# A hybrid encoder block on one core: two centred LayerNorm cells kept on chip, new lane rates, a fifth raw weight buffer, and roots a call later

## The chip, the cores and the metric

The kernel runs on one NeuronCore of a Trainium2 chip. Its engines are named here as the profile names them: TensorE (PE, its weight loads PEld), VectorE (DVE), ScalarE (ACT), GpSimd (POOL) and SyncE (SP), which issues most DMAs. The metric is the device time of one execution, in microseconds (us).

## The reference

One layer over 2048 tokens of 1024 channels, in float32:

```
h = rmsnorm(x)
u_pool(512) | u_glu(2x512) | g_a(1024) | g_b(1024) = h @ w_in
A = ((trailing_mean(u_pool, 2/4/8/16) - u_pool) @ pool_w per group * pool_scale) @ w_pool_out
v = depthwise_conv31(a * sigmoid(gate)) + conv_b            # 512 channels, causal
B = silu(layernorm(v) * ln_g + ln_b) @ w_conv_out
x = x + rmsnorm((sigmoid(g_a) * A + sigmoid(g_b) * B) @ w_o)
x = x + rmsnorm(relu(rmsnorm(x) @ w_up)^2 @ w_down)
```

## The kernel before

**Number format and tiling.** Every float32 operand is split into a high and a low half of a faster format (`split`, `split_w`: ScalarE casts the high half, VectorE subtracts for the low one), and three of the four half products are summed. Each matrix product of 2 x 2 blocks is done with seven block products and sums of blocks (`Octet`, products numbered 1 to 7, in the sequence `START`, then `ORDER`). One such product is 24 matmuls of 128x128 by 128x512 into one accumulator of 1024 columns in PSUM. There are 385 of them: glu, pool, ga and gb (the input projection), A and B (the two branches), wo, up and down. Tokens go in two halves of 1024 (`b` = 0, 1).

**Weights.** `load_w` loads a raw weight tile into a buffer of pool `wr` (four), ScalarE casts it to `wh`. The low half `wl` is made by VectorE at first use and stored in DRAM (`kept`); at the second use it is loaded from there, `wl<-kept`.

**What sets the order.** TensorE runs the products in one main line. Other work is written as generators (`conv_steps`: 31 depthwise taps, one VectorE instruction each, L918; `pool_steps`; `norm_steps`, the LayerNorm; `pool_weights`, which folds w_pool into w_pool_out; `mlp_scale`, the sums of squares for the mlp's norm). A `Lane` calls them after each product: its `rate` is added to a credit, each step costs one, and a `yield n` has the lane skip n - 1 calls. Within `behind()` each instruction of a step is bound not to be placed before the main line's last one. The scheduler lays out each engine's instructions in an order fixed in the program; `high_priority(offset=...)` brings instructions forward in it. An engine runs its list in order and waits at the first instruction that is not ready. So do the DMA queues: SP's list holds nearly all loads and most stores (`load`, L129), ScalarE's some stores (`store`, L137), POOL's a few transfers (`aside`, and those that accumulate).

**The norm.** `norm_steps` subtracts the mean from four cells (a cell is 128 channels by 1024 tokens), stores each centred cell to DRAM (`yd`), sums squares, has TensorE make the root's sum (`root_acc`, L458) and spread it, loads the four cells again, and makes z, which goes to DRAM as `zd`. z is the operand of the B products. `yd` also carries the convolution's result to the norm.

**Roots.** A root is eight or sixteen matmuls of one column, put between TensorE's product matmuls. `mlp_scale` runs for the second half while the up products run; its squares lie in buffers named fo.

**Sums.** Every second product or so, a sum of two accumulators is made: ScalarE copies one out of PSUM (`held`, L408), VectorE adds the other (`tr<-gb,tr`, L120), and the accumulator is free again after that. Three accumulators exist.

Of the kernel before, what the change touches and what calls it, by code (L numbers as in the profile page):

```python
# [15 lines left out]
P = 128  # L16
# [52 lines left out]
def block_kernel(  # L69
# [20 lines left out]
    p_const = pool("const", 1)  # L90
    p_dram = pool("dram", 1, space=bass.MemoryType.DRAM)
    p_sm = pool("psm", 2)
    p_wr = pool("pwr", 4)
    p_ws = pool("pws", 2)
    p_wh = pool("pwh", 3)
    p_wl = pool("pwl", 3)
# [31 lines left out]
    def load(o, src):  # L128
        return nc.sync.dma_start(o, src)  # L129
# [308 lines left out]
                self.sink(1, 0, ps, None)  # L438
            bg()

    def run_octets(octets, bg):

        jobs = [(octets[k], i) for k, i in START]
        jobs += [(o, i) for o in octets[2:] for i in ORDER]
        for n, (o, i) in enumerate(jobs):
            o.run(i, jobs[min(n + (2 if n > 3 else 1), len(jobs) - 1)][1], bg)
            if n == 3:
                o.raw.clear()

# [446 lines left out]
    def conv_steps(b, groups, ahead=True):  # L896
# [8 lines left out]
        for c in groups:  # L905
# [24 lines left out]
            load(yd[b, c, 0], acc)  # L930
            yield

    def norm_steps(b, lag):

        yield 3
        sh, sl = split(sums[b], *TR)
        yield 3
        mu = mk(p_ss, "r", F32, (P, W))[:, :TB]
        y = {}

        def prefetch(c):
# [12 lines left out]
        ss = mk(p_ss, "sm")  # L954
        for c in range(CC):
            if c + 2 < CC:
                prefetch(c + 2)
            sub(y[c], y[c], mu)
            load(yd[b, c, 0], y[c])
            sq = ss if c == 0 else tr()  # L960
            nc.scalar.activation(sq, y[c], AF.Square)
            if c % 2:
                yield 1
            if c:
                add(ss, ss, sq)
        yield lag
        r = mk(p_ss, "r", F32, (P, W))[:, :TB]
        halves = [ss[:, t * T : (t + 1) * T] for t in (0, 1)]

        def got(t, rb):  # L970
            nc.scalar.copy(r[:, t * T : (t + 1) * T], rb)

        yield from inv_rms_steps(halves, inv_c, TR, lag, got)
        prefetch(0)
        yield 1
        sg = {}
        for c in range(CC + 1):
            if c < CC:
                if c + 1 < CC:
                    prefetch(c + 1)  # L980
                mul(y[c], y[c], r)
                sg[c] = tr()
                nc.scalar.activation(
                    sg[c], y[c], AF.Sigmoid, scale=col(C_LG + c), bias=col(C_LB + c)
                )
                nc.scalar.activation(
                    y[c], y[c], AF.Identity, scale=col(C_LG + c), bias=col(C_LB + c)
                )
            if c:
                mul(y[c - 1], y[c - 1], sg[c - 1])  # L990
                load(zd[b, c - 1, 0], y[c - 1])
            yield 1

    pw = [p_const.tile([P, CW], F32R, tag=f"pw{i}", name=f"pw{i}") for i in (0, 1)]

    w_pp = [dram("wpp", (P, D)) for _ in range(CPS)]

    def pool_weights():

        yield 2  # L1000
        raw = tr()
        load(raw[:, :CW], w_pool)
        for g in range(CC):
            part = raw[:, g * P : (g + 1) * P]
            nc.scalar.activation(part, part, AF.Copy, scale=col(C_PSC + g))
        nc.scalar.copy(pw[0], raw[:, :CW])
        sub(pw[1], raw[:, :CW], f32(pw[0]))
        yield

        def get(g):  # L1010
            t = tr()
            load(t, w_po[g])
            return t

        for g, t in ahead_by_one(range(CC), get):
            hi, lo = split(t, *TR)
            yield 3
            ps = psum("mix")
            for h in (0, 1):
                n = slice(h * T, (h + 1) * T)  # L1020
                matmuls(ps[:, n], pw, g, [(hi[:, n], lo[:, n])], main=False)
            w = tr()
            nc.scalar.copy(w, ps)
            yield
            for c in range(CPS):
# [346 lines left out]
    def mlp_scale(b, buf):  # L1372

        st = None
        for t in (0, 1):
            sq = Squares(buf)
            for c in range(0, CPS, 2):
                x = [mk(*buf) for _ in (0, 1)]
                for i in (0, 1):
                    load(x[i], x1d[b, c + i, t])  # L1380
                yield 1
                sq.add(x[0])
                sq.add(x[1])
            yield 1
            ss = sq.total()
            yield 1
            if st is None:
                st = root_psum()
            root_acc(st, ss, inv_d, t * G)
# [8 lines left out]
    def mlp_up(b, parts):  # L1398
        def one(u):
# [3 lines left out]
            def sink(m, t, ps, s):  # L1403
                o = tr()
                if s is not None:
                    mark(add(o, ps, s))
                    ps = o
                mark(nc.scalar.activation(o, ps, AF.Relu))
                nc.scalar.activation(o, o, AF.Square)
# [74 lines left out]
            lane.empty()  # L1484
        lanes.clear()

    def run(*octets):
        run_octets([o for group in octets for o in group], bg)

    parts = Parts(first_parts)  # L1490
    first_octet()
    parts.need(6)
    o2, = glu(0, parts, ahead_raw[:1])
    tail = Lane(1.3, conv_steps(0, (0,)))
    stats = Lane(1, in_stats(1))
    weights = Lane(2, pool_weights())

    def then(f, o, at=4):
# [20 lines left out]
    then(lambda: lanes.append(stats), o2, 5)  # L1519
    run(  # L1520
        [o2],
        [then(more, pi, 3)],
        gate(0, parts, 3, sad, "ga", "lows"),
        gate(0, parts, 5, sbd, "gb", "sums"),
    )
    stats.empty()
    weights.empty()
# [19 lines left out]
    def pooling():  # L1547
# [9 lines left out]
        g1[0],  # L1557
        g1[1],
        gate(1, parts, 5, sbd, "gb", "sums"),
    )  # L1560
    conv1 = lanes.pop()
    empty()
# [224 lines left out]
    class Finish:  # L1787
# [144 lines left out]
        for i in FIRST:  # L1932
            fill[i] = token_cells(0, i, 0, (p_fo, "fo"))

    def filler(part):
        for i in FIRST:
            for o in (0, 1):
                w = part(i, o)
                ps = psum("down")
                product(ps, w, fill[i])  # L1940
# [18 lines left out]
    filler(weights_down(0))  # L1959
# [5 lines left out]
    run(octs)  # L1965
    empty()
    part = {}
    coming = got
# [97 lines left out]
```

## Time and profile before

| | us |
|---|---|
| median of 3 executions (lowest to highest) | 2214.71 (2211.72 to 2218.5) |
| the profiled execution | 2215.49 |
| its span, first to last instruction | 2213.7 |
| TensorE busy | 2165.7 |
| VectorE busy | 1677.5 |
| ScalarE busy | 1040.2 |
| moved by DMA | 567.51 MB, mean 256 GB/s |

The profile is of one execution. A row of the timeline gives the start, the length, the engine, the line, the instruction as out<-in, how many were merged into the row, and, in brackets, how long the engine stood idle before and what released it. The list of waits gives a sum, how many, and the longest. The table of stretches gives, for each, its length, the busy time and count of each engine shown, the granted TensorE clock (PEclk), the share of DMA engines busy and GB/s; where one engine alone is asked for, the first pair is that engine's.

### The profile page before, as it was taken

The page shows a single profiled execution, that of the slowest core. Times are in us where ns is not written, and L with a number is a line of the kernel's source. Part 1 is how long each engine was busy: PE and PEld are TensorE (multiplying, and loading weights), DVE is VectorE, ACT ScalarE, POOL GpSimd, SP SyncE. Part 2 cuts the span into 40 slices and gives each one's busy share as a digit, 9 for nine tenths or more (in the row PEclk, how much of TensorE's full clock was granted, in tenths as well). Part 3 has the DMA queues.
Part 4 walks back from the last instruction along what each step waited for, and adds up shares of the span by engine and source line. Part 5 has one row for each costly group of instructions (what it writes and reads, how often), then busy time and mean ns, then how long its engine had stood idle before and what let it go on. Part 6 is the DMA issues. An engine that isn't in the chain of part 4 may idle for free.

```text
span 2213.7 us, 25020 instructions
## 1 busy us (share of the span) xinstructions
PE 2165.7 (98%) x9556; PEld 1784.4 (81%) x9556; DVE 1677.5 (76%) x1633; ACT 1040.2 (47%) x1098; POOL 20.6 (1%) x39
## 2 busy tenths in 40 slices
PE   9999999999999999999999999999999999999996
PEld 7788787887888788888888877888888888888875
DVE  8998998987778888967657856876754656696667
ACT  5444353334533445456535766664554222223553
POOL 0000000000000000000000000000000000000001
PEclk9999999999999999999999999999999999999998
DMA  4779897678986688365686677985966545446798
GB/s 166 275 291 344 305 366 282 236 278 310 351 323 238 252 311 310 123 218 189 229 306 236 247 267 266 329 317 197 372 213 233 181 156 189 149 146 219 266 319 248
DMA packets 162791, 567.51 MB, mean 256 GB/s; under 512 B 18896, under 2 KB 23120, under 8 KB 162640
## 3 DMA queue, kind: packets, MB, share of 16 engines
q1 hardware_dynamic: 145968, 505.09, 64.1%
q10 hardware_dynamic: 12672, 46.14, 5.3%
q0 software_dynamic: 4032, 14.68, 2.5%
q8 instruction: 75, 1.23, 0.2%
q14 instruction: 44, 0.36, 0.0%
HBM read 376.49 MB, written 190.41 MB: 256 GB/s over the span
## 4 chain that ended last, share of the span: by engine, by line
PE 76%; DVE 9%; DMA 9%; issue 2%; ACT 2%; SPq 0%; DVEq 0%; ACTq 0%; POOL 0%; POOLq 0%
PE down L252 26%; PE up L252 22%; PE glu L252 6%; PE wo L252 6%; PE B L252 4%; PE A L252 4%; PE ga L252 3%; PE gb L252 3%; PE pool L252 2%; DVE y L918 2%; DVE wl L123 1%; DMA tr<-yd 1%; DVE tr L120 1%; DMA fo<-x1d 1%; DMA kept<-ws 1%
## 5 line engine op out<-in xcount | busy, mean ns | idle before, releaser
L252 PE MATMUL up<-big,wh 128*128 128x512 f32 x1792 | 482.4, 390 | 2.1 <-DVE big L123 1.8
L252 PEld LDWEIGHTS up<-big,wh 128*128 128x128 f32 x1792 | 337.0, 188 | 74.5 <-DVE big L123 3.9
L209 ACT CAST wh<-wr 128x1024 fp32r<-128x1024 f32 x169 | 177.5, 1051 | 324.1 <-PE up L252 77.8
L252 PE MATMUL down<-tr,wh 128*128 128x512 f32 x800 | 311.7, 390 | 0.0
L918 DVE SCALAR_TENSOR_TENSOR y<-v,cst,y 128x1024 f32<-128x1024 f32 x240 | 307.3, 1281 | 2.8
L252 PE MATMUL down<-fo,wh 128*128 128x512 f32 x784 | 301.8, 390 | 0.0
L252 PE MATMUL up<-big,wl 128*128 128x512 f32 x896 | 277.2, 390 | 0.0
L252 PE MATMUL down<-fo,wl 128*128 128x512 f32 x768 | 236.8, 390 | 2.9 <-DMA wl<-lows 2.9
L209 ACT CAST wh<-ws 128x1024 fp32r<-128x1024 f32 x118 | 124.2, 1052 | 221.8 <-PE up L252 84.1
L252 PEld LDWEIGHTS up<-big,wl 128*128 128x128 f32 x896 | 168.3, 188 | 34.7
L120 DVE TENSOR_TENSOR big<-big,down 128x1024 f32<-128x1024 f32 x88 | 106.8, 1218 | 111.9 <-PE down L252 104.0
L1727 ACT CAST fo<-tr 128x1024 fp32r<-128x1024 f32 x86 | 86.8, 1051 | 210.0 <-PE down L252 132.1
L252 PEld LDWEIGHTS down<-tr,wh 128*128 128x128 f32 x800 | 150.6, 188 | 31.2
L252 PEld LDWEIGHTS down<-fo,wh 128*128 128x128 f32 x784 | 147.5, 188 | 30.6
L252 PEld LDWEIGHTS down<-fo,wl 128*128 128x128 f32 x768 | 144.1, 188 | 33.2 <-DMA wl<-lows 3.3
L123 DVE TENSOR_TENSOR wl<-ws,wh 128x1024 fp32r<-128x1024 f32 x110 | 134.2, 1220 | 32.7 <-ACT wh L209 31.5
L123 DVE TENSOR_TENSOR wl<-wr,wh 128x1024 fp32r<-128x1024 f32 x99 | 120.5, 1218 | 27.9 <-ACT wh L209 26.8
L123 DVE TENSOR_TENSOR tr<-tr,fo 128x1024 fp32r<-128x1024 f32 x86 | 101.8, 1220 | 46.5 <-ACT fo L1727 46.5
L252 PE MATMUL wo<-big,wh 128*128 128x512 f32 x480 | 128.9, 390 | 0.0
L252 PE MATMUL gb<-big,wh 128*128 128x512 f32 x448 | 121.0, 392 | 3.0 <-DVE tr L120 2.4
L252 PE MATMUL glu<-big,wh 128*128 128x512 f32 x432 | 120.2, 400 | 3.5 <-DVE big L123 1.8
L252 PE MATMUL ga<-big,wh 128*128 128x512 f32 x448 | 120.9, 392 | 0.0
(197 smaller groups left out, 3349.1 us busy)
## 6 DMA issues: line engine op xcount, KB each, us to landing
tr<-fd SPq DMA_DIRECT2D x110, 512.0 KB, 4.6
wl<-kept SPq DMA_DIRECT2D x81, 512.0 KB, 4.8
kept<-wl SPq DMA_DIRECT2D x74, 512.0 KB, 5.7
wr<-w_down SPq DMA_DIRECT2D x68, 512.0 KB, 5.2
wr<-w_up SPq DMA_DIRECT2D x64, 512.0 KB, 4.6
wr<-w_in SPq DMA_DIRECT2D x56, 512.0 KB, 5.4
fd<-tr ACTq DMA_DIRECT2D x54, 512.0 KB, 3.6
fd<-tr SPq DMA_DIRECT2D x48, 512.0 KB, 3.5
```

The lines of the kernel that those rows point to most:

```text
L120: return nc.vector.tensor_tensor(o, a, b, op=ALU.add)
L123: return nc.vector.tensor_tensor(o, a, b, op=ALU.subtract)
L209: nc.scalar.copy(hi[:, :n], src[:, :n])
L252: i = nc.tensor.matmul(ps, w[wp][:, (at + k) * P : (at + k + 1) * P], rhs[k][xp], start=start and n == 0, stop=stop and n == len(order) - ...
L918: nc.vector.scalar_tensor_tensor(acc, v[:, k : k + TB], wk, acc, op0=ALU.mult, op1=ALU.add)
L1727: nc.scalar.copy(hi, t)
```

## The change

- Pool `wr` of raw weights has five buffers instead of four.
- `norm_steps` keeps the centred cells 2 and 3 on chip (HELD): they are neither stored to `yd` nor loaded again. The second pass takes them first, then cells 0 and 1, which it asks for up to two ahead.
- The two halves of w_pool, constants before, are a temporary of one `tr` buffer, and `pool_weights` skips a call more.
- `mlp_scale` skips one call more before its root, and `mlp_up`'s sum of two accumulators is scheduled with an offset of 60.
- The convolution's lane starts after glu's second octet (`o2`) has done its product 1, one product later than before, at rate 1 instead of 1.3, later 2.5 instead of 3; the rest of its work is appended two products earlier. The second half's lane goes to 2.2 instead of 3.4.
- `run_octets` takes from which product on it looks two products ahead for operands: 3 as before, but 2 in the last `mlp_up`.
- The plain `out` store in `mul_left` goes through POOL's queue instead of SP's.

No instruction of TensorE, VectorE or ScalarE is added or removed. Eight transfers of 0.5 MB go.

```diff
-    p_wr = pool("pwr", 4)
+    p_wr = pool("pwr", 5)
...
-    def run_octets(octets, bg):
+    def run_octets(octets, bg, early):
...
-            o.run(i, jobs[min(n + (2 if n > 3 else 1), len(jobs) - 1)][1], bg)
+            o.run(i, jobs[min(n + (2 if n > early else 1), len(jobs) - 1)][1], bg)
...
+    HELD = (CC - 2, CC - 1)
+
     def norm_steps(b, lag):
...
             sub(y[c], y[c], mu)
-            load(yd[b, c, 0], y[c])
+            if c not in HELD:
+                load(yd[b, c, 0], y[c])
...
         yield from inv_rms_steps(halves, inv_c, TR, lag, got)
-        prefetch(0)
+        order = HELD + tuple(c for c in range(CC) if c not in HELD)
+        ready = list(HELD)
+
+        def ask(n):
+            if n < CC and order[n] not in ready:
+                prefetch(order[n])
+                ready.append(order[n])
+
+        ask(0)
         yield 1
         sg = {}
-        for c in range(CC + 1):
-            if c < CC:
-                if c + 1 < CC:
-                    prefetch(c + 1)
+        for n in range(CC + 1):
+            if n < CC:
+                c = order[n]
+                ask(n + 1)
+                ask(n + 2)
                 mul(y[c], y[c], r)
...
-            if c:
-                mul(y[c - 1], y[c - 1], sg[c - 1])
-                load(zd[b, c - 1, 0], y[c - 1])
+            if n:
+                c = order[n - 1]
+                mul(y[c], y[c], sg[c])
+                load(zd[b, c, 0], y[c])
             yield 1
-
-    pw = [p_const.tile([P, CW], F32R, tag=f"pw{i}", name=f"pw{i}") for i in (0, 1)]
...
         raw = tr()
+        both = mk(*TR, F32R)
+        pw = both[:, :CW], both[:, CW:]
...
             hi, lo = split(t, *TR)
-            yield 3
+            yield 4
...
             ss = sq.total()
-            yield 1
+            yield 2
             if st is None:
                 st = root_psum()
             root_acc(st, ss, inv_d, t * G)
...
                 if s is not None:
-                    mark(add(o, ps, s))
+                    with tc.high_priority(offset=60):
+                        mark(add(o, ps, s))
...
-    tail = Lane(1.3, conv_steps(0, (0,)))
+    tail = Lane(1, conv_steps(0, (0,)))
...
+    def after_glu():
+        ahead[0] = AHEAD
+        lanes.append(tail)
+
     def more():
         ahead[0] = AHEAD
         lanes.append(weights)
         tail.gens.append(chain_of(pool_steps(0, True), conv_steps(0, (1, 2, 3), False)))
-        tail.rate = 3
+        tail.rate = 2.5
...
     ahead[0] = 45
-    lanes.append(tail)
     then(lambda: lanes.append(stats), o2, 5)
     run(
-        [o2],
-        [then(more, pi, 3)],
+        [then(after_glu, o2, 1)],
+        [then(more, pi, 5)],
...
     def faster():
-        conv1.rate = 3.4
+        conv1.rate = 2.2
...
-                    load(out[self.b, c, self.t], y)
+                    nc.gpsimd.dma_start(out[self.b, c, self.t], y)
...
-    run(octs)
+    run(octs, early=2)
```

The other lines of the diff pass `early=3`, or hand the fill-in products of down their weights as arguments, with the same work.

The scheduler's order shows what moves. VectorE, the gb products of the first half (y is the convolution's accumulator, wl a low weight half, ws a sum of weights). Before:

```order
L120 TENSOR_TENSOR tr_2084<-gb_2058,tr_2046 128x1024
L123 TENSOR_TENSOR wl_2189<-ws_2186,wh_2188 128x1024
L918 SCALAR_TENSOR_TENSOR y_2005<-v_1957,cst,y_2005 128x1024 x3
L123 TENSOR_TENSOR ws_2227<-wr_2051,ws_2097 128x1024
L918 SCALAR_TENSOR_TENSOR y_2005<-v_1957,cst,y_2005 128x1024 x2
L123 TENSOR_TENSOR wl_2230<-ws_2227,wh_2229 128x1024
L918 SCALAR_TENSOR_TENSOR y_2005<-v_1957,cst,y_2005 128x1024 x2
L123 TENSOR_TENSOR wl_2269<-wr_2093,wh_2268 128x1024
L918 SCALAR_TENSOR_TENSOR y_2005<-v_1957,cst,y_2005 128x1024 x2
L120 TENSOR_TENSOR tr_2220<-gb_2020,tr_2181 128x1024
```

With the change:

```order
L120 TENSOR_TENSOR tr_2073<-gb_2047,tr_2028 128x1024
L123 TENSOR_TENSOR wl_2162<-ws_2159,wh_2161 128x1024
L123 TENSOR_TENSOR ws_2213<-wr_2040,ws_2084 128x1024
L914 TENSOR_SCALAR y_2156<-v_2119,cst 128x1024
L123 TENSOR_TENSOR wl_2216<-ws_2213,wh_2215 128x1024
L918 SCALAR_TENSOR_TENSOR y_2156<-v_2119,cst,y_2156 128x1024
L123 TENSOR_TENSOR wl_2254<-wr_2080,wh_2253 128x1024
L120 TENSOR_TENSOR ws_2371<-wr_2367,wr_2369 128x1024
L123 TENSOR_TENSOR ws_2373<-ws_2371,wr_2290 128x1024
L120 TENSOR_TENSOR tr_2193<-gb_2002,tr_2154 128x1024
```

Between the first and the second add of gb stand nine taps before, and two steps of the convolution with the change.

SP's queue where the first half's last products (A, pool) end and those of the second begin (kept, wsum and the like are in DRAM). Before:

```order
L129 DMA wl_2990<-kept_795 128x1024
L129 DMA wr_3188<-kept_1256 128x1024
L129 DMA kept_2878<-wl_2875 128x1024
L129 DMA mad_136<-tr_2833 128x1024
L129 DMA wr_3224<-kept_1215 128x1024
L129 DMA wl_3027<-kept_293 128x1024
L129 DMA wl_3063<-kept_276 128x1024
```

With the change (kept_291 is the tile that was kept_293):

```order
L129 DMA wr_3168<-kept_1251 128x1024
L129 DMA wl_2933<-kept_826 128x1024
L129 DMA kept_2774<-wl_2771 128x1024
L129 DMA mad_134<-tr_2729 128x1024
L129 DMA kept_2856<-wl_2853 128x1024
L129 DMA wl_2968<-kept_791 128x1024
L129 DMA mad_135<-tr_2766 128x1024
L129 DMA wr_3204<-kept_1209 128x1024
L129 DMA wl_3005<-kept_291 128x1024
```

The low half wl_3027 (wl_3005) stands behind the raw load of wr_3224 (wr_3204) in both. That load's buffer was used four raw loads earlier before, and five with the change, whose own raw load ahead of it (wr_3168) also stands further up.

TensorE at the first root of `mlp_scale`, within an up product. Before:

```order
L252 MATMUL up_10367<-big_9845,wl_10454 128x512
L252 MATMUL up_10367<-big_9841,wh_10453 128x512
L458 MATMUL rb_10438<-inv_d,fo_10299 128x1 x4
L252 MATMUL up_10367<-big_9842,wh_10453 128x512
L252 MATMUL up_10367<-big_9841,wh_10453 128x512
```

With the change:

```order
L252 MATMUL up_10354<-big_9828,wh_10431 128x512
L252 MATMUL up_10354<-big_9829,wh_10431 128x512
L252 MATMUL up_10354<-big_9828,wh_10431 128x512
L252 MATMUL up_10354<-big_9829,wh_10431 128x512
L252 MATMUL up_10354<-big_9832,wh_10431 128x512
L252 MATMUL up_10354<-big_9833,wh_10431 128x512
L252 MATMUL up_10354<-big_9828,wl_10432 128x512 x2
L252 MATMUL up_10354<-big_9832,wl_10432 128x512
L252 MATMUL up_10354<-big_9832,wh_10431 128x512
L252 MATMUL up_10354<-big_9833,wh_10431 128x512
L252 MATMUL up_10354<-big_9832,wl_10432 128x512
L458 MATMUL rb_10474<-inv_d,fo_10286 128x1 x4
```

The root moved 11 matmuls down, to the product's end. On ScalarE, at the down products at about 1609 us, the copy of an accumulator (`big<-down`, L1738) stands behind two casts `fo<-big` before, and between them with the change.

More of the change, by code (lines that the diff above doesn't have):

```diff
@@ L1485, in empty, with run @@
         lanes.clear()
-    def run(*octets):
-        run_octets([o for group in octets for o in group], bg)
+    def run(*octets, early=3):
+        run_octets([o for group in octets for o in group], bg, early)
     parts = Parts(first_parts)
@@ L1513, in more @@
         tail.gens.append(chain_of(pool_steps(0, True), conv_steps(0, (1, 2, 3), False)))
-        tail.rate = 3
+        tail.rate = 2.5
     pi = pool_in(0, parts, ahead_raw[1])[0]
     ahead[0] = 45
-    lanes.append(tail)
     then(lambda: lanes.append(stats), o2, 5)
     run(
-        [o2],
-        [then(more, pi, 3)],
+        [then(after_glu, o2, 1)],
+        [then(more, pi, 5)],
         gate(0, parts, 3, sad, "ga", "lows"),
         gate(0, parts, 5, sbd, "gb", "sums"),
+        early=3,
     )
@@ L1559, in block_kernel @@
         gate(1, parts, 5, sbd, "gb", "sums"),
+        early=3,
     )
@@ L1589, in faster @@
     def faster():
-        conv1.rate = 3.4
+        conv1.rate = 2.2
     octs = mlp_up(0, parts)
     then(faster, octs[1])
-    run(octs)
+    run(octs, early=3)
     empty()
@@ L1933, in fill_cells, with filler @@
             fill[i] = token_cells(0, i, 0, (p_fo, "fo"))
-    def filler(part):
+    def filler(part, halves):
         for i in FIRST:
-            for o in (0, 1):
+            for o in halves:
                 w = part(i, o)
@@ L1958, in block_kernel @@
     lanes += [Lane(1, chain)]
-    filler(weights_down(0))
+    fw = weights_down(0)
+    filler(fw, (0, 1))
     octs = mlp_up(1, parts)
@@ L1964, in block_kernel @@
         then(lambda n=n: got.append(token_cells(*jobs[n], BIG, BIG if n == 2 else None)), octs[-1], i)
-    run(octs)
+    run(octs, early=2)
     empty()
```

## The prediction

> **What bounds the kernel now.** I read the page's first two parts first.
>
> ```profile
> span 2213.7 us, 25020 instructions
> PE 2165.7 (98%) x9556; PEld 1784.4 (81%) x9556; DVE 1677.5 (76%) x1633; ACT 1040.2 (47%) x1098; POOL 20.6 (1%) x39
> ```
>
> TensorE is busy for 98% of the span, and the change gives it the same 385 products of 24 matmuls, in the same sequence. So its work is fixed, and only places where it stands still, or runs at a low clock, can move the time. The list of TensorE's waits names them:
>
> ```profile
> PE rb L458 <- DVE fo L120: 4.7, 3, 1.6
> PE glu L252 <- DMA wl<-kept: 4.0, 1, 4.0
> PE down L252 <- DMA wl<-lows: 2.9, 1, 2.9
> PE gb L252 <- DVE tr L120: 2.4, 2, 2.0
> PE glu L252 <- DVE big L123: 1.8, 1, 1.8
> PE rb L458 <- DVE sm L120: 1.7, 1, 1.7
> PE pool L252 <- DVE tr L120: 1.3, 2, 0.7
> PE gb L252 <- ACT tr L408: 0.6, 1, 0.6
> ```
>
> A wait here is idle time only. What a place really loses is counted from the busy-time table of TensorE in stretches: the first row is an undisturbed one, 441 matmuls in 100 us, 0.2268 us each; a stretch's length less its count times 0.2268 is its loss.
>
> ```profile
> 150.00:250.00 100.00, 99.99 (x441) 1.00 0.92 334
> 94.00:112.00 18.00, 14.75 (x50) 0.81 0.87 331
> 254.00:272.00 18.00, 15.97 (x63) 0.91 0.77 291
> 358.00:378.00 20.00, 15.98 (x64) 0.91 0.80 285
> 1284.00:1294.00 10.00, 9.04 (x38) 1.00 0.69 235
> 2126.00:2142.00 16.00, 13.08 (x51) 0.89 1.03 392
> ```
>
> The losses are 6.7 (94), 3.7 (254), 5.5 (358), 1.4 (1284) and 4.4 us (2126). Four places hold a root, whose short matmuls TensorE runs between two products. There I take the same table for the line of the products alone (L252), so that the root's own time has to be taken off too:
>
> ```profile
> 522.00:540.00 18.00, 14.53 (x57) 0.91 0.79 291
> 1364.00:1378.00 14.00, 11.47 (x44) 0.88 0.81 303
> 1424.00:1438.00 14.00, 11.57 (x51) 1.00 0.91 336
> 1454.00:1468.00 14.00, 11.50 (x52) 1.00 0.93 358
> ```
>
> The lengths less the counts leave 5.1, 4.0, 2.4 and 2.2 us. An mlp_scale root (1364, 1424, 1454) itself takes 0.9 (in the timeline from 1369.10 to the next product matmul at 1370.01), the norm's root at 522 1.8, so 3.3, 3.1, 1.5 and 1.3 are lost.
>
> The clock column says why 1364 lost twice as much as 1424 for about the same wait (1.6 and 1.5 us): at 1364 the granted clock was 0.88. A stall somewhere above 1.6 us is followed by a half-speed stretch that costs a further 1.5 us; one of 1.5 is not. The Trainium skill ("TensorE: Matmul & The Clock Gate", "What's actually happening") has the clock halve only after an idle window of about 3.4 us; here the stalls of 2.0 and 1.6 us already show it, so the measurement decides, and I price a stall of 2 us or more at its length plus 1.5.
>
> **The change part by part.** The sum is made against the profiled execution, 2215.5 us for its span of 2213.7, which lies 0.8 over the median of 2214.7.
>
> *Lane rates (tail at 1, then 2.5; started by o2's first product).* The product at 258 us waits until VectorE has added an earlier sum out of PSUM. VectorE's and TensorE's timelines:
>
> ```profile
> 253.28 2.60 DVE L918 SCALAR_TENSOR_TENSOR y<-v,cst,y 128x1024 f32<-128x1024 f32 x2
> ...
> 256.93 2.60 DVE L918 SCALAR_TENSOR_TENSOR y<-v,cst,y 128x1024 f32<-128x1024 f32 x2
> 259.44 1.22 DVE L120 TENSOR_TENSOR tr<-gb,tr 128x1024 f32<-128x1024 f32 x1
> 260.72 1.78 PE L252 MATMUL gb<-big,wh 128*128 128x512 f32 x6 [2.03 <-DVE tr L120]
> ```
>
> Conv taps (L918), 1.28 us each, stand ahead of the add. Between the first and second gb add there are nine taps now, and two conv steps in the change; seven taps, 9 us, go, while the add was 2.0 us late. Counted with the trace's durations over the order, VectorE then owes the lane up to some 24 us of work; it pays that back between about 480 and 632 us. The stall at 258 goes, and the one that repeats at 301 us (0.4): gain 4.0 (3.5 to 4.1). At 94 us one tap fewer stands ahead of the operand's low half, which was 1.8 us late; the rest of that stall is ScalarE's and VectorE's own chain: gain 2, from 0 to 4.5. The short waits of pool (1.3 in two) and of gb on ScalarE's copy (0.6) have the same cause or lie behind norm work that moves: 1.1 of 1.9.
>
> *A fifth raw weight buffer.* At 361 us a low weight half came late. From TensorE's and SP's timelines:
>
> ```profile
> 366.66 0.97 PE L252 MATMUL glu<-big,wl 128*128 128x512 f32 x3 [4.02 <-DMA wl<-kept]
> 359.40 0.32 SPq L129 DMA_DIRECT2D wr<-kept  x1
> 359.76 3.79 SPq L129 DMA_DIRECT2D wl<-kept  x3
> ```
>
> SP issues in order. The low half at 359.76 stood behind a load into a raw buffer (359.40), which waited for ScalarE's cast of that buffer's last owner. With five buffers the owner is one product older, so the load, and the low half behind it, can go some 5 us earlier, as soon as TensorE has freed the low buffer. Gain 4.8 of 5.5 (3.5 to 5.5): 4.0 of waiting is covered by a step of one product, 24 times 0.2268 = 5.4 us.
>
> *mlp_scale's extra call, and the sink's priority.* The roots at 1367, 1428 and 1458 stand before VectorE's final add:
>
> ```profile
> 1368.36 0.68 DVE L120 TENSOR_TENSOR fo<-fo 128x512 f32<-128x512 f32 x1
> 1369.10 1.05 PE L458 MATMUL rb<-inv_d,fo 128*128 128x1 f32 x8 [1.61 <-DVE fo L120]
> ```
>
> The add ended at 1369.04; the root now stands at the end of that product, 11 matmuls or 2.5 us later than 1367.3, at 1369.8. That leaves 0.8 us; at the other three places I find 0.4 to 1.8. Gain 5.0 of the 5.9 lost, 3 if one of them still stalls by 1.5 and its clock drops.
>
> *norm_steps.* In either half of the tokens, two of the four centred cells are no longer stored and loaded again: eight transfers of 0.5 MB less, of 567 MB in all. No TensorE time is freed by that. But the norm's root moves seven products on, behind a VectorE add that is then ready early: 2.7 of 3.3 at 522 (0.5 to 3.3). What can be late next is the z that the first B product needs:
>
> ```profile
> 613.42 3.49 DVE L123 TENSOR_TENSOR big<-big,big 128x1024 fp32r<-128x1024 f32 x3
> 631.90 1.52 PE L252 MATMUL B<-big,wh 128*128 128x512 f32 x6
> DMA to landing us min/median/max: 2.8/5.6/7.8
> ```
>
> Before, z's halves are made from 613 on, 12 us ahead of use. In the change z's reloads (landing row, of tile zd) are issued only at about 616, land at 619 to 624, and the last half is made at about 632.5, where it is needed at about 634. Loss between 0 and 5 (a landing at 7.8 with a queue in front and the low clock); I take 1.5, nearer to the median's landing.
>
> *Run-ahead of the last mlp_up (early=2).* An operand is split one product sooner, at 1286: gain 1.0 of 1.4. *fold's weights in a temporary* move no engine's work; nothing.
>
> *Order of ScalarE at 1609 us.* The scheduler now puts a copy ahead of a cast whose halves the next product needs:
>
> ```profile
> 1608.34 1.05 ACT L1727 CAST fo<-big 128x1024 fp32r<-128x1024 f32 x1 [2.43 <-DVE big L120]
> 1609.39 1.02 ACT L1738 COPY big<-down 128x1024 f32<-128x1024 f32 x1
> 1610.71 0.50 PE L252 MATMUL down<-big,wh 128*128 128x512 f32 x1 [0.23 <-DVE big L123]
> ```
>
> The copy starts when the product before ends (1609.4), the cast then at 1610.3 to 1611.4, VectorE's low half at 1612.6: TensorE goes on 1.9 us later. The stall is then over 2 us, so 1.9 to 3.4; I take 3.
>
> *Two out stores to POOL's queue.* They are the last of their kind:
>
> ```profile
> 2193.49 10.75 SPq L129 DMA_DIRECT2D out<-big  x7
> 2197.56 0.89 POOL L1911 DMA_DIRECT2D out<-big  x1 [10.52 <-DVE big L126]
> ```
>
> SP's tail of stores gets shorter, POOL's two accumulating stores come about 1.1 us later (0.9 for each issue); the last packets of both queues end close together. -1 to +1.5; I take 0.
>
> The stall at 2126 stays: there SP's load of lows is held behind two other out stores, whose place does not change. So does the root at 772. Small shifts (a spread at 583, the roots' slack): 0.6 lost.
>
> Gains 4.0 + 2.0 + 1.1 + 4.8 + 5.0 + 2.7 + 1.0 = 20.6; losses 1.5 + 3.0 + 0.6 = 5.1; net 15.5, about 2200 from the profiled execution and 2199 from the median.
>
> **The rivals.**
>
> *z becomes the new wait.* For it: the late reloads. Against: the median landing fits. Price: 5 for z, and 3 of the norm's 2.7 and the slack lost: 2199 + 6, 2203 to 2209.
>
> *The stalls only move.* The change does not do what it says if VectorE is as full where it repays the lane as it was at 258. VectorE's busy time stands third in these rows:
>
> ```profile
> 250.00:300.00 50.00, 47.97 (x205) 39.20 (x204) 49.47 (x43) 22.94 (x24) 0.00 (x0) 0.97 0.90 325
> 500.00:550.00 50.00, 48.33 (x214) 39.77 (x213) 36.38 (x45) 21.91 (x24) 0.00 (x0) 0.97 0.88 308
> 550.00:600.00 50.00, 49.39 (x219) 40.55 (x218) 38.23 (x32) 27.63 (x27) 0.00 (x0) 1.00 0.95 346
> ```
>
> Between 480 and 632 us 24 us come in addition, 8 in each 50: 44 to 46, not 49. If it happens all the same, three or four late sums at 3.7 give back 11 to 15: 2210 to 2214, no change.
>
> *Slower.* The same repayment falls in one lump, in front of the ga adds from 478 us on. For it: by the order the eight products from there carry some 51 us of VectorE work in 43.5 us (24 x 0.2268 each). From the point where VectorE has no free time in 50 us, each sum there comes as late as that at 258, at 3.7 us; seven of them make 26: 2225. Against: the products just before leave it some 5 us free, and an accumulator is needed again only some products after its sum.
>
> *The skill's window.* By the clock page's 3.4 us, the low clock at 254, 522 and 1364 would not be due to the stalls that go. Then their 1.5 each stays, and 1609 costs 1.5 less: 2199 + 4.5 - 1.5 = 2202. The rows are against it.
>
> **How the numbers follow.** The forecast 0.55, with 2192 to 2206 of its own; z 0.18; no change by moved stalls 0.13; slower 0.08; the window 0.06. Executions before lie from 2211.7 to 2218.5, so 0.3%, 6.6 us, is what can be told from nothing. Faster by more (below 2208): 0.55 + 0.06 + most of z's, 0.18 = 0.79; same 0.13; slower 0.08. For 8 in 10 the range runs from 2191 (all gains at their upper ends with the low losses, 24.7, would be 2190) to 2211, which takes in z's case and the lower part of the moved stalls'.
>
> **What would show it.** In the changed profile: no wait of glu on wl<-kept over 1 us; gb on DVE tr under 0.5; rb on DVE fo under 1; a new wait of down on DVE or ACT near 1609 of 2 us; B on DVE big at about 632 of 0 to 5; VectorE at 44 to 46 of 50 in 500 to 600. A list of TensorE's waits as long as before, with new names, would prove the forecast wrong.

## The result, and the profile after

The changed kernel takes 2198.2 us (median of 6, 2196.0 to 2204.2) against 2213.2 (median of 6, 2207.7 to 2218.5) for the kernel before: a ratio of 0.9936, 95% interval 0.9920 to 0.9952. That is 14 us, 11 to 18, faster. In the later rounds of runs the kernel before had medians of 2210.0 to 2210.6 (11 to 31 executions each); against those the same 2198.2 would be some 12 us faster, so 14 may be a little high. The forecast was 2199, with 2191 to 2211. The total was right. What the experiments then showed is that the terms behind it were not: hardly any was a gain that its edit brings by itself.

The first rows of the page after:

```profile
span 2194.5 us, 25001 instructions
PE 2158.8 (98%) x9556; PEld 1782.7 (81%) x9556; DVE 1679.3 (77%) x1633; ACT 1040.3 (47%) x1098; POOL 21.8 (1%) x41
```

The compute instructions of TensorE, VectorE and ScalarE are the same in number. From TensorE's list of waits after, whose rows sum to about 21 us where they summed to about 30 before:

```profile
PE rb L550 <- DVE sp L530: 4.5, 2, 3.4
PE glu L252 <- DVE big L123: 2.9, 2, 2.2
PE rb L458 <- DVE tr L120: 2.7, 3, 1.4
PE down L252 <- DMA wl<-lows: 2.6, 1, 2.6
PE down L252 <- ACT fo L1746: 1.1, 1, 1.1
PE pool L252 <- DVE wl L123: 1.1, 1, 1.1
...
PE gb L252 <- ACT tr L408: 0.8, 1, 0.8
...
PE down L252 <- DVE big L123: 0.8, 1, 0.8
...
PE rb L458 <- DVE sm L120: 0.3, 1, 0.3
```

Gone are glu on wl<-kept (4.0), gb on VectorE (2.4) and rb on VectorE fo (4.7). TensorE's stretches around the same products (first pair TensorE's busy time and count, then its clock):

```profile
94.00:112.00 18.00, 14.05 (x53) 0.91 0.85 317
252.00:270.00 18.00, 18.00 (x82) 1.00 0.88 313
350.00:370.00 20.00, 19.70 (x87) 1.00 0.99 358
725.00:741.00 16.00, 12.62 (x53) 0.89 0.37 131
```

The second and third, the places of the old stalls at 258 and 361 us, are full to within 0.3 us, at clock 1.00. The first still loses most of what it lost. The last is a new stall that nobody had foreseen.

A finer ledger comes from the start of each product's first matmul in the two traces: 5.44 us from one to the next where nothing disturbs. A root that has moved has its own time in another product, so such places are summed over both.

| place (us in the trace before) | before | after | gained | predicted |
|---|---|---|---|---|
| 92 to 115, glu and pool, three products | 23.66 | 22.77 | 0.9 | 2.0 |
| 253, gb, two products | 14.85 | 10.88 | 4.0 | 4.0 |
| 361, glu | 11.38 | 5.44 | 5.9 | 4.8 |
| 521 and 566, the norm's root, seven products | 45.29 | 42.31 | 3.0 | 2.7 |
| 1281, up, two products | 12.69 | 10.88 | 1.8 | 1.0 |
| 1364 to 1484, mlp_scale's roots | | | 7.0 | 5.0 |
| 632, first B product | 5.44 | 5.44 | 0 | -1.5 |
| 742, wo | 6.91 | 11.62 | -4.7 | not foreseen |
| 1609, down | 5.96 | 7.91 | -2.0 | -3.0 |
| last product's start to the span's end | 34.9 | 33.0 | 1.9 | 0 |

These make 17.8 of the 19.2 us between the two spans; the rest is small shifts. In these two executions, then, the forecast holds place by place in its signs. The sizes come out larger: the eight places that it priced give 20.6 us, not 15.0, and the place that it did not foresee takes 4.7 back. Had I stopped here, I would have said that each edit did its part.

How far one pair of executions can be trusted is seen where two traces hold the same program. The kernel e5 below has the instructions of the kernel before in the same order on every engine and queue, by the profile's names, up to 1367 us. Its three products at 92 take 23.4 us, the two at 253 take 15.2, the one at 361 takes 10.3, much as before (23.7, 14.9, 11.4). But its seven products of the norm take 40.9, not 45.3. So the 3.0 us gained at the norm's place lie within what one program scatters there, and are not shown to be a gain.

### The profile page after: what moved, and what is told of

Read it like the earlier page. It is cut to its first block, busy times and chain, and to the rows that moved or that the text cites. A ratio compares the mean times of both kernels' runs of the same rounds, so it can differ in the third digit from the quotient of the medians.

```text
span 2194.5 us, 25001 instructions
## 1 busy us (share of the span) xinstructions
PE 2158.8 (98%) x9556; PEld 1782.7 (81%) x9556; DVE 1679.3 (77%) x1633; ACT 1040.3 (47%) x1098; POOL 21.8 (1%) x41
## 4 chain that ended last, share of the span: by engine, by line
PE 87%; DVE 5%; DMA 5%; ACT 1%; issue 1%; SPq 0%; DVEq 0%; ACTq 0%; POOLq 0%
PE up L252 28%; PE down L252 26%; PE ga L252 7%; PE wo L252 6%; PE gb L252 6%; PE glu L252 5%; PE B L252 4%; PE pool L252 3%; PE A L252 2%; DVE y L918 1%; DMA kept<-wl 1%; PE rb L458 1%; DVE tr L120 1%; DVE big L126 1%; DVE big L123 1%
## 5 line engine op out<-in xcount | busy, mean ns | idle before, releaser
L252 PE MATMUL ga<-big,wh 128*128 128x512 f32 x448 | 119.8, 389 | 0.0
```

The source lines that it names most:

```text
L252: i = nc.tensor.matmul(ps, w[wp][:, (at + k) * P : (at + k + 1) * P], rhs[k][xp], start=start and n == 0, stop=stop and n == len(order) - ...
```

## The experiments

All ratios are to the kernel before, with 95% intervals.

| kernel | ratio | interval | median, us |
|---|---|---|---|
| the change | 0.9936 | 0.9920 to 0.9952 | 2198.2 |
| before + fifth buffer (e1_wr5) | 0.9969 | 0.9953 to 0.9985 | 2206.7 |
| before + lanes (e3_lanes) | 1.0001 | 0.9987 to 1.0016 | 2210.8 |
| before + later roots (e5_yield2) | 1.0014 | 1.0001 to 1.0026 | 2213.5 |
| before + fifth buffer and lanes (e14_wr5lanes) | 0.9961 | 0.9948 to 0.9974 | 2202.9 |
| change, four buffers (e2_wr4) | 1.0000 | 0.9985 to 1.0016 | 2212.1 |
| change, old lanes (e4_oldlanes) | 0.9962 | 0.9945 to 0.9978 | 2201.1 |
| change, no cells kept (e6_nohold) | 0.9929 | 0.9906 to 0.9952 | 2193.8 |
| change, old roots (e10_noyield2) | 0.9944 | 0.9927 to 0.9961 | 2198.1 |
| change, out store on SP (e8_outsp) | 0.9940 | 0.9922 to 0.9958 | 2196.3 |
| change, four buffers, tr<-yd on POOL (e11_wr4_ydpool) | 0.9992 | 0.9978 to 1.0005 | 2209.5 |
| e6 and the first half's out stores on POOL (e12_best) | 0.9967 | 0.9954 to 0.9981 | 2204.9 |
| e6 and out store on SP (e15_lean) | 0.9942 | 0.9929 to 0.9956 | 2195.9 |

From each kernel's one profile, the same ledger at seven places (us, by the starts of products; the places in the time of the kernel before; roots are counted with the products they stand in, so that the norm's column holds both of its places). Four groups of matmuls of w_pool's fold, 1.4 us each, stand between the products of the first column; in e4 one of the four stands among the two at 253 instead, so that its 12.2 holds no stall and its 102.1 is one group short:

| kernel | 154 to 253, 17 products | 253, 2 | 361, 1 | the norm's, 7 | 1281, 2 | mlp_scale's, 20 | 1609, 1 |
|---|---|---|---|---|---|---|---|
| before | 98.7 | 14.9 | 11.4 | 45.3 | 12.7 | 119.7 | 6.0 |
| the change | 98.4 | 10.9 | 5.4 | 42.3 | 10.9 | 112.7 | 7.9 |
| e1, buffer alone | 103.5 | 10.9 | 5.4 | 41.8 | 12.6 | 114.8 | 9.5 |
| e3, lanes alone | 104.6 | 11.0 | 5.4 | 44.2 | 12.7 | 115.7 | 6.1 |
| e5, roots alone | 99.0 | 15.2 | 10.3 | 40.9 | 12.7 | 119.8 | 6.0 |
| e14, buffer and lanes | 102.2 | 10.9 | 5.4 | 43.7 | 12.7 | 116.2 | 9.5 |
| e2, four buffers | 100.7 | 11.0 | 5.4 | 47.1 | 10.9 | 118.3 | 9.6 |
| e4, old lanes | 102.1 | 12.2 | 5.4 | 40.8 | 10.9 | 112.7 | 7.9 |
| e6, no cells kept | 98.4 | 10.9 | 5.4 | 42.0 | 10.9 | 112.7 | 7.9 |
| e10, old roots | 98.4 | 10.9 | 5.4 | 42.2 | 10.9 | 113.5 | 7.9 |

### The fifth buffer, alone and taken away

```diff
-    p_wr = pool("pwr", 4)
+    p_wr = pool("pwr", 5)
```

(with w_pool's halves in a temporary, for the room; the second kernel is the change with 4 again.)

> The kernel before with the fifth raw weight buffer alone (and w_pool's halves in a temporary, which makes the room). Theory 'buffer': the low half at 361 us was late only because a raw load ahead of it on SP waited for a buffer. Then TensorE's wait of glu on wl<-kept (4.0 us) is gone, the product there takes 5.4 us instead of 11.4, all other waits stay as before (gb on VectorE 2.4, rb on VectorE fo 4.7), and the time falls by 5 to 6 us. Rival 'emptier VectorE': the load came earlier in the changed kernel because VectorE and ScalarE were earlier there. Then the wait stays at 3 us or more and the time is that of before.

> The changed kernel with four raw weight buffers again. Theory 'buffer': a wait of glu (or of the product next to it) on wl<-kept of 3 to 4 us comes back near 358 us and the time rises by 4 to 6 us, to about 2203. Rival 'emptier VectorE': no such wait, 2198.

Alone it gains 0.31%, 7 us, about what was expected. But its ledger has more places than the one: the product at 361 takes 5.44 us, the two at 253 take 10.88 too, the norm's products take 3.5 less (within the scatter that e5 shows there), and mlp_scale's twenty products 4.9. It pays for that with new stalls: 4.7 us at 160, where ga waits for ScalarE's copy, and 3.6 at the down product of 1609. The first rows of its waits:

```profile
PE rb L458 <- DVE tr L120: 4.5, 4, 2.0
PE ga L252 <- ACT tr L408: 3.2, 1, 3.2
...
PE rb L458 <- DVE fo L120: 1.6, 2, 1.4
```

Taken away from the change, it costs all 14 us: the ratio is 1.0000, with 2212.1 against the change's 2198.2. And the wait that I had tied it to, glu on wl<-kept at 361, does not come back. Both theories for that place fall short: the buffer is enough to remove that stall (e1), and so are the lanes without it (e3, below). What comes back stands elsewhere. Against the change's trace, the products at 284 and 291 lose 5.4 us more, those at 549 and 557, with the norm's root, 4.8 more, and mlp_scale's twenty 5.6 more.

Around the norm's root, SP's and TensorE's rows in the change:

```profile
539.56 0.33 SPq L129 DMA_DIRECT2D wr<-w_in  x1
539.99 0.40 SPq L129 DMA_DIRECT2D tr<-yd  x1
...
543.09 0.44 SPq L129 DMA_DIRECT2D tr<-yd  x1
555.30 1.95 PE L458 MATMUL rb<-inv_c,sm 128*128 128x1 f32 x16 [0.31 <-DVE sm L120]
```

and with four buffers:

```profile
546.97 0.33 SPq L129 DMA_DIRECT2D wr<-w_in  x1
547.40 0.40 SPq L129 DMA_DIRECT2D tr<-yd  x1
...
552.41 0.33 SPq L129 DMA_DIRECT2D wr<-w_in  x1
552.80 0.46 SPq L129 DMA_DIRECT2D tr<-yd  x1
564.28 3.40 PE L458 MATMUL rb<-inv_c,sm 128*128 128x1 f32 x16 [1.88 <-DVE sm L120]
```

With four buffers each tr<-yd goes out right behind a raw weight load, and the queue's own list of waits has what the load at 552.41 waited for, ScalarE's cast out of a raw buffer (550 to 553 us):

```profile
SPq L129 <- ACT wh L209: 2.2, 1, 2.2
```

With five, such waits sum to 0.5 us between 539 and 543.6, and the scheduler has also put the last tr<-yd ahead of the next raw load. Against the product whose root needs it, which starts at 549.4 and 556.8, the last one goes 6.3 us ahead with five buffers and 4.0 with four, and the whole chain on VectorE follows it. At 284 us it is ScalarE that is held. With four buffers:

```profile
281.76 0.80 SPq L129 DMA_DIRECT2D wr<-wpp  x2
282.61 0.42 SPq L129 DMA_DIRECT2D kept<-ws  x1
292.54 1.23 DVE L123 TENSOR_TENSOR ws<-wr,ws 128x1024 f32<-128x1024 f32 x1 [2.55 <-DMA kept<-ws]
293.80 1.05 ACT L209 CAST wh<-ws 128x1024 fp32r<-128x1024 f32 x1 [6.22 <-DVE ws L123]
297.94 2.68 PE L252 MATMUL gb<-big,wh 128*128 128x512 f32 x6 [4.60 <-ACT tr L408]
```

The store of ws leaves SP behind two raw loads; VectorE waits for it before it writes ws again; ScalarE's cast waits for VectorE; the copy of gb stands behind the cast; and TensorE waits 4.6 us for the accumulator. In the change the store left at 276.23, 8.0 us before the product at 284.26 began, not 5.1 (282.61 to 287.74), and TensorE waited 0.8. So the fifth buffer's worth is not in the one low half that I had priced; at these two places it is in what stands on SP behind raw loads.

### The same cause from the other side: tr<-yd off SP's queue

```diff
             y[c] = tr()
-            load(y[c], yd[b, c, 0])
+            aside(y[c], yd[b, c, 0])
```

> The changed kernel with four raw buffers, and the norm's loads tr<-yd issued by POOL's queue instead of SP's. With four buffers the norm's root waited 1.9 us at 562 us and its products lost 4.8 us; tr<-yd stood on SP right behind loads into raw buffers. Theory 'what stands behind a raw load on SP is late': the root's wait falls under 0.7 and the two products lose 1 us or less, while the stall of gb on ScalarE at 290 us (kept<-ws, still on SP) stays; about 2207 against 2212 with four buffers. Rival 'the loads are late for the DMA engines' sake': the root's wait stays at 1.5 to 2.5 and the time at 2212.

With four buffers, but the norm's loads on POOL's queue, the root starts without a wait, and its two products lose 5.4 us less:

```profile
560.71 1.84 PE L458 MATMUL rb<-inv_c,sm 128*128 128x1 f32 x16
...
PE gb L252 <- ACT tr L408: 5.0, 2, 4.4
```

The stall behind kept<-ws, still on SP, stays at 4.4. Both went as the theory had it. In the norm's steps between 540 and 565 us VectorE waited four times for tr<-yd with four buffers, 5.9 us in all; here it does not wait for one. The time, 2209.5, is 2.6 below that with four buffers, but the two intervals overlap, so the total does not show a gain. The rows bear out that standing behind raw loads on SP made these loads late. They come from one execution of each kernel, and e5 shows 4.4 us of scatter at the norm's place in one program, so this is strong support and not proof. Busy DMA engines are not the reason: their share between 540 and 565 us was 0.96 with four buffers and 0.97 here.

### The lanes, alone and taken away

```diff
-    tail = Lane(1.3, conv_steps(0, (0,)))
+    tail = Lane(1, conv_steps(0, (0,)))
...
-        tail.rate = 3
+        tail.rate = 2.5
...
-        [then(more, pi, 3)],
+        [then(after_glu, o2, 1)],
+        [then(more, pi, 5)],
```

> The kernel before with the new lane rates and starts alone. Theory 'lanes make room at the front': gb's wait on VectorE at 258 us (2.0, with the low clock 4.0 lost) is gone and 0 to 2 us of the stall at 98 us; the norm's root at 526 us keeps its wait of 1.7, since I put that gain down to the norm's own code; the time falls by 4 to 6 us. Rival 'lanes do both': the norm comes later with its lane, its root's wait goes too, 7 to 9 us. Rival 'stalls only move': the sum of TensorE's waits stays within 1 us of before's.

> The changed kernel with the old lane rates and starts. The fifth buffer alone already took away the stalls at 258 and 361 us, so two theories stand against each other. 'The buffer gives all': the lanes add nothing, 2198 as the changed kernel, gb's wait at 258 us stays away. 'They work together': taps are ahead of the gb adds again, a wait of gb or ga on VectorE or ScalarE of 2 us or more comes back between 160 and 300 us, and the time rises by 4 to 7 us, to 2202 to 2205.

Alone the lanes gain nothing (1.0001). Yet their ledger has all that was expected and more: 253 and 361 lose next to nothing, the norm's root moves on by seven products, mlp_scale's lose 4 us less, the three products at 92 lose 2.8 less. The rival "stalls only move" has it, and by more places than I had in mind: 154 to 253 loses 5.9 us more, and further products 1.0 to 2.3 us each, at 289, 564 and 847 us of its own trace. The rows of TensorE's list sum to about 31 us, where before's sum to about 30. Some of them:

```profile
PE gb L252 <- ACT tr L408: 3.5, 2, 2.1
PE up L252 <- DVE big L123: 3.4, 4, 1.6
PE pool L252 <- DVE tr L120: 2.1, 2, 1.5
PE ga L252 <- DVE tr L120: 2.1, 1, 2.1
PE ga L252 <- ACT tr L887: 1.8, 1, 1.8
```

Taken away from the change, they cost some 3 us by the medians, 2201.1 against 2198.2, and 6 by the ratios, where 4 to 7 were expected. The two differ because the kernel before was faster in this round (2210.1) than beside the change (2213.2). And ga waits again on ScalarE's copy (3.2) at 160 us, as with the fifth buffer alone. The intervals overlap, so that they add something over the buffer is likely, and not shown. The buffer and the lanes alone (e14) come to 2202.9:

> The kernel before with two edits alone: the fifth raw weight buffer (w_pool's halves in a temporary) and the new lane rates and starts. Theory 'these two carry the change': 2194 to 2200, ratio 0.992 to 0.9955, no wait of rb on VectorE fo over 1.5 us although mlp_scale's roots stand where they did. Rival 'the other edits add up to some 5 us': 2202 to 2205.

That lies in the rival's range: the other edits are worth some 5 us. The ledger says where. With both edits alone, 154 to 253 us loses 3.8 more than in the change. There fold's own products stand between the ga and gb products, and of the edits that e14 lacks only `pool_weights`' further call acts there, which I had not priced. 1281 loses 1.8: every kernel with early=2 has 10.9 there and every kernel without it (all built from the kernel before) 12.6 to 12.7, so this term (1.0, measured 1.8) was probably right in kind, and short. mlp_scale's products lose 3.5 more.

### mlp_scale's roots, alone and taken away

```diff
             ss = sq.total()
-            yield 1
+            yield 2
```

(the second kernel also has the sink's add without its priority.)

> The kernel before with mlp_scale's extra call before its roots alone, without the sink's priority. Theory: the three waits of rb on VectorE fo (4.7 us) fall under 1, four roots stand later, 6 to 7 us less (the trace's product lengths put the loss there at 7.0, the table of stretches at 5.9). Rival 'the priority is needed as well': VectorE's final adds move back too, a root still waits 1 to 2 us and the gain is 2 to 4.

> The changed kernel with mlp_scale's roots and the sink's add as before. In the kernel before, the later roots alone gained nothing, because a copy behind the fold of w_down on ScalarE stalled up for 3 us at 1400 us. Theory 'with five buffers the roots are worth their stalls': rb on VectorE fo waits 3 to 5 us again, the time rises by 4 to 6 us to 2202 to 2204. Rival 'roots are worth nothing': 2198, the stalls just stand at other places.

Alone they cost 0.14%, at the edge of its interval. The three roots do lose most of their waits, and two products at 1392 take 6.0 us more, 0.9 of it a root that moved there; in sum, the twenty products take what they took (119.8). ScalarE's and TensorE's rows there:

```profile
1397.37 1.06 ACT L587 ACTIVATE fo<-fo 128x1024 f32<-128x1024 f32 x1 [3.91 <-DVE fo L123]
...
1400.22 0.99 ACT L408 COPY tr<-up 128x1024 f32<-128x1024 f32 x1
1401.27 2.93 PE L252 MATMUL up<-big,wh 128*128 128x512 f32 x6 [3.24 <-ACT tr L408]
```

The copy stands behind the squares, and these behind a fold of w_down on VectorE that waits for its load. Taken away from the change, the later roots are hardly missed: 2198.1, and 2 us by the ratios, well within the intervals. For line L458 the profile gives what TensorE (its weight loads with it) waited for. Before, and in the change with the old roots:

```profile
  DVE fo L120: 10.9, 7
```

```profile
  DVE fo L120: 1.9, 4
```

With the roots at their old place the wait is gone all the same. So the theory "with five buffers the roots are worth their stalls" falls; the predicted 5.0 was removed by something else. The ledger names the edit: taking the buffer away from the change brings 5.6 us of it back (118.3 against 112.7), taking the lanes away brings none (112.7). The way from the buffer to these products stays open. It is not the raw loads alone: in the three traces in which TensorE waits there for the copy, all with four buffers and later roots, SP waited for a store out of an fo buffer before it issued a load of the fold: 2.9 us in e11, 3.6 in e2 (1385 to 1390) and 5.8 in e5 (1386 to 1393). The last two as rows:

```profile
SPq L129 <- DMA wsum<-fo: 3.6, 1, 3.6
...
SPq L129 <- DMA wsum<-fo: 5.8, 1, 5.8
```

### Cells kept on chip, and the out store

```diff
-            if c not in HELD:
-                load(yd[b, c, 0], y[c])
+            load(yd[b, c, 0], y[c])
```

> The changed kernel with norm_steps as before (all four centred cells stored and loaded again). Theory: keeping two cells frees no time on TensorE by itself; z has more slack at the first B product and the norm's roots stay where the lane puts them; within 2 us of the changed kernel (2196 to 2200). Rival 'the eight transfers matter': loads behind them on SP come later, 3 to 5 us more, with a wait of TensorE on DMA or on tr<-yd's users between 520 and 640 us.

> The changed kernel with the plain out store on SP's queue again. From the last VectorE instruction to the span's end it took 10.9 us before and 7.4 us in the changed kernel. Theory of the prediction: the queue is worth -1 to 1.5 us, 2197 to 2200, and the end of 7.4 us comes from chance. Rival 'the store on POOL shortened the end': 10 to 11 us again from the last VectorE instruction to the end, 2201.

Without HELD: 2193.8. With the out store on SP: 2196.3. Both times are a little under what was expected. Neither edit gains; the eight transfers that HELD saves are not missed. From VectorE's last instruction to the span's end it takes 7.4 to 10.8 us with POOL's store (six kernels, e12 left out) and 8.8 to 10.9 with SP's (seven kernels): the 1.9 us gained at the end are mostly within that scatter. Both edits undone together:

> The changed kernel without HELD and with the plain out store on SP's queue, so without two of its edits that gained nothing when they were undone alone. Theory 'both are worth nothing': 2192 to 2198, ratio 0.991 to 0.9955. Rival 'the best time without HELD (2193.8) came from POOL's store, or from chance': 2199 or more.

2195.9, ratio 0.9942: not to be told from the change. The change is as fast with two of its edits less. No kernel here beats it beyond the intervals.

### An attempt at the last large wait

```diff
                 nc.gpsimd.dma_start(y, x1d[self.b, c, self.t], accum_op=ALU.add)
-                load(out[self.b, c, self.t], y)
+                nc.gpsimd.dma_start(out[self.b, c, self.t], y)
```

> The changed kernel without HELD (norm_steps as before), and with the plain out stores behind the accumulating POOL transfers in the first half's finish on POOL's queue as well. The last large wait of TensorE, down on wl<-lows (2.6 to 5.2 us in all kernels so far, with the low clock 4.5 to 7.7 lost), comes from SP's list: the load stands behind two out stores that wait for POOL's transfer to land. Theory: that wait is gone, 4 to 5 us less than the changed kernel without HELD (2193.8), 2188 to 2190. Rival 'something else on SP is next': the wait goes to tr<-fd or wr<-wsum behind it and the gain is under 2 us.

The product that lost up to 7.7 us now takes 5.44, and the next one 14.9. TensorE there:

```profile
2117.43 0.74 PE L252 MATMUL down<-fo,wl 128*128 128x512 f32 x2 [2.64 <-DMA wl<-lows]
...
2126.45 1.87 PE L458 MATMUL rb<-inv_d,tr 128*128 128x1 f32 x8 [3.03 <-DVE tr L120]
```

The rival was right that the wait moves, though not where to, and it is worse than it said: the load of lows is late one product on, a root waits 3 us besides, and 2204.9 is 11 us more than without the edit (8 by the ratios). What makes the root's add late there was not followed up.

## Why the prediction was right, and where it was not

**The bound.** "Only places where TensorE stands still or runs at a low clock can move the time" held in all kernels: same work, medians from 2194 to 2213 us.

**The places.** Seven of the eight were called with the right sign, most within 1 to 2 us in the profiled pair; the norm's place is not told from scatter. That 20.6 us at these places against 15.0 forecast still ended near 2199 owes something to luck: the stall at 742, which no step of the forecast had, took 4.7 of the surplus in this execution. The z chain had slack enough: the first B product took 5.44 us, the low bound of its range. The order of ScalarE at 1609 cost 2.0, near the low bound of 1.9: the stall came as two waits, 1.1 on ScalarE and 0.8 on VectorE, and the stretch there kept its clock:

```profile
1588.00:1600.00 12.00, 10.09 (x44) 1.00 0.94 354
```

The kernel with the out store on SP (e8) has the same two waits, 1.1 and 0.8, at the same products in the same order, and there the clock fell and the product took 9.5 us, not 7.9:

```profile
1582.00:1594.00 12.00, 10.10 (x36) 0.86 0.94 351
```

**The price of a stall.** The prediction took a stall of 2 us or more at its length plus 1.5. In the trace before, that reading rests on waits of 1.58 us (clock kept) and 1.61 us (clock lost), and the other traces do not bear it out. Ten kernels have a wait of 2.2 us in glu at 101 to 103 us: seven lose their clock in 94 to 112 us (0.91), three keep it at 1.00. Two of them, e15 and e6, have the same order there and the same 2.19 us of waiting:

```profile
94.00:112.00 18.00, 14.48 (x60) 1.00 0.89 326
...
94.00:112.00 18.00, 14.29 (x54) 0.91 0.85 317
```

Six matmuls, 1.4 us, lie between them. So 1.5 is right as the price of a clock that falls, but a wait's length does not say whether it will. The gain of 2.0 at 94 us came out as 0.9 in the change's profile, with a low clock, and would be 3.0 by e8's (20.7 us for the three products), without one.

**The sizes.** I took losses from counts of matmuls in a stretch. Such a count is good to one matmul, 0.23 us, and three short stretches gave 5.9 for the roots where product starts give 7.0. The starts are the better ruler.

**VectorE's repayment.** I said 44 to 46 busy of 50 in 500 to 600 us. It was 39 and 41:

```profile
500.00:550.00 50.00, 50.00 (x222) 41.41 (x221) 39.35 (x33) 22.27 (x24) 0.00 (x0) 1.00 0.83 303
550.00:600.00 50.00, 49.69 (x228) 41.12 (x227) 40.97 (x49) 30.22 (x30) 0.00 (x0) 1.00 0.84 321
```

The taps that the lane put off were largely done before 500: of the convolution's taps between 100 us and there, 120 had run before and 115 with the change, where at 400 it had been 84 and 69. None of the rivals that hung on this came about.

**The step that failed is the sum itself.** It added terms, each with its edit, as if the edit moved its own place and no other. Undone one at a time, the terms are 14 us for the fifth buffer (put at 4.8), 3 to 6 for the lanes (put at 7.1), 0 to 2 for the roots (put at 5.0) and 0 or less for the norm's cells (2.7). Added one at a time, the first three are 7, 0 and -3. One resource, the raw buffers, stood behind several of the stalls, at two of them by way of SP's list, and more than one edit could take away the same stall (361 went with the buffer alone and with the lanes alone). A total worked out from stalls of the trace can be right while the list of causes is wrong.

**What stays open.** Why either edit at the front alone opens new stalls between 154 and 253 us, which the whole change does not have; whether fold's further call closes them was not tried by itself, nor were early=2 and the sink's priority. How the fifth buffer helps mlp_scale's products is open too, and the change was not run again beside the kernels of the later rounds.

## What to carry to other kernels

Where a queue issues in order and some of its loads wait for a buffer, price another buffer by everything that stands behind those loads, and look for it on every engine's waits. In a program whose order is made by a scheduler, an edit's gain is known only by taking it out again: undo each part, since parts added alone gave 7, 0 and -3 us of 14. A ledger of product starts shows a moved stall that totals hide; but before a place of one profile is read as a gain, look at the same place in a second trace of the same order.

## What the runs showed of the hardware that I had not expected

Of the kernel before, executions ran from 2205 to 2219 us; that spread, 0.6%, is as large as the whole gain. One way in which it arises is in the trace of the change. VectorE waits for the store of a channel (yd<-y) before it may write y again, and small steps of a root stand behind the taps. VectorE's and TensorE's rows after, and the same instruction before:

```profile
716.30 0.81 DVE L914 TENSOR_SCALAR y<-v,cst 128x1024 f32<-128x1024 f32 x1 [7.34 <-DMA yd<-y]
...
733.09 0.33 PE L550 MATMUL rb<-ident,sp 128*128 128x128 f32 x1 [3.38 <-DVE sp L530]
```

```profile
727.05 0.81 DVE L914 TENSOR_SCALAR y<-v,cst 128x1024 f32<-128x1024 f32 x1 [4.19 <-DMA yd<-y]
```

The store was issued at 707.2 and VectorE went on at 716.3, 9.1 us later; before it was 6.6 (720.4 to 727.0). With these 2.5 us, and an issue that was 0.7 later against TensorE's products, VectorE went on 3.2 us later; TensorE waited 3.4 us and lost its clock: 4.7 us. In all thirteen other profiles here that product takes 6.4 to 7.5 us, so this was that execution, not the change. One late landing of a store cost 4.7 us, a third of the 14 that the whole change gains.

The low clock is a second way. Three waits recur in many of the kernels, and the same wait is followed by a low clock in some and not in others: 2.2 us at 101 to 103 us (seven of ten), 1.4 us before a root at 759 to 773 us (five of ten, the product taking 9.2 to 9.6 us with it and 8.0 without), and 1.1 to 1.2 with 0.8 us at the down product of 1609 (four of eleven). Which it will be in an execution, the lengths of these waits do not tell; why, no run here shows.
